# Encoder layer with mLSTM and dilated attention: another DRAM layout of the attention queries and keys, and loads of 128 partitions for wide attention units

## The chip, the cores and the metric

The program runs on one core of a Trainium2 chip. The time is device microseconds of one execution; of several executions the median is given. Times inside the program come from one profiled execution. PE is TensorE, DVE VectorE, ACT ScalarE, POOL GpSimd, SP the engine that does nothing but issue transfers (DMA).

## The reference

One layer of a bidirectional encoder is applied to two sequences, a prompt of 1024 tokens and a sample of 512, both 1024 wide, with the same weights. A common projection feeds an mLSTM branch (4 heads of 256) and an attention branch of three groups (window, dilation) with 8 heads of 64 each; both are gated, projected, merged, projected again and normed. The part that the change touches is the attention's queries and keys:

```python
A_PATTERNS = ((128, 1), (512, 4), (2048, 16))
...
for g, (win, dil) in enumerate(A_PATTERNS):
    o, mx, den = dilated_group(qkv[:, :, 0, g] * (A_HEAD_DIM ** -0.5), qkv[:, :, 1, g], qkv[:, :, 2, g],
                               dil, win // (2 * dil), rel_table[:, g])
...
logits = jnp.einsum('bghnqe,bghnke->bghnqk', qr, kb) + bias[:, None]
logits = jnp.where(mask, logits, -jnp.inf)
mx = jnp.max(logits, axis=-1)
p = jnp.exp(logits - mx[..., None])
o = jnp.einsum('bghnqk,bghnke->bghnqe', p, vb)
```

## The kernel before

The program first projects the prompt (A) and stores what the branches need in DRAM, then runs the branches of A and of the sample (B). During the branches PE is kept busy with the remaining dense products ("fill"): the sample's projection and the output projections.

*Projection of the prompt.* Columns are made in units of 128 (two heads of 64), two units at a time, by seven products of half size (`unit_pair`, products `d<-Hh,phla` and `phlb` at L212 to L214, 19 us a pair). Their weights `pw_raw` are loaded by SP at L692, split into a high and a low part by ACT and DVE (L678, L679) and summed by POOL (L697 to L715). `att_unit` (L770) takes the 24 query and key units, queries (0 to 11) first. For groups 0 and 1 it makes a high part (`hi`, a copy) and a low part (`lo`, the rest), and stores each as 128 rows of 1024 floats into the DRAM tensor `aqk_a` (L222, 512 KB a store). Group 2 has one part only. The sample's units go to `aqk_b` from tiles `sw` while the mLSTM of A runs.

*Attention.* `attend` (L1801) goes through 12 units: unit u is group u // 4, heads 2 (u % 4) and the next. A unit is *wide* when its sequence by residue is longer than 128: groups 0 and 1 of the prompt (units 0 to 7) and group 0 of the sample (units 0 to 3). A wide unit makes the logits of a tile with four products (L1695, `lg<-V0a,Q` and so on): for each head, the query tile, 64 rows of the high part and 64 of the low part in one tile of 128 rows, with a key tile of the same high part twice, and again with a key tile of the low part beside zeros. So `att_load` (L1484) fills, per head, a query tile `Q` from two places of 64 rows, the key tile `V0a` or `V1a` with the same 64 rows in both halves, and half of the tile `V0b` or `V1b` with the low part: five loads of 64 rows a head, ten a unit. Even units use V0, odd ones V1.

*Order of the transfers.* In the branches PE and SP run in the order in which the code is written; DVE, ACT and POOL are ordered by the compiler's scheduler. `att_load` puts its loads into a list (`queue`, L241). `spread(rounds)` sets how many of them go out per step (the length of the list over the rounds, rounded up), `tick` (L234) issues that many at each step, and `need` (L247) issues the rest of a group when its unit begins. All go through `fetch` (L253) to SP. Stores of results wait in a second list (`put`, `flush`, L228). A unit's loads are asked for from the second step of the unit before it. The first unit's loads are asked for during the mLSTM's last head, and stand there ahead of that head's gate loads (`X<-G_a`) in the same list. The fill's weights (`wraw`, L264) go through SP or POOL.

Of the kernel before, what the change touches and what calls it, by code (L numbers as in the profile page):

```python
# [22 lines left out]
F32 = mybir.dt.float32  # L23
# [6 lines left out]
P = 128  # L30
# [9 lines left out]
DILS = (1, 4, 16)  # L40
# [33 lines left out]
class Tokens:  # L74


    def __init__(self, dram, S, x, y, name):
        self.S, self.x, self.y, self.n, self.nblk, self.name = S, x, y, S // P, S // BLK, name
        t = lambda shape, what, dt=F32: dram.tile(shape, dt, name=f"{what}_{name}")
        self.qk = t([16, P, S], "qk")  # L80
        self.vs = t([2, S, D], "vs")
        self.G = t([8, P, S], "G")
        self.aqk = t([2, 24, P, S], "aqk")
        self.av = t([S, 1536], "av")
        self.az = t([4, P, S], "az")
        self.gt = t([2, 8, P, S], "gt")
        self.rw = t([8, self.n, 2, P], "rw")
        self.ym = t([12, P, S], "ym")
        self.og = t([S, 3, 4, OW], "og")


class Rot:
# [91 lines left out]
class Net:  # L184
# [585 lines left out]
    def att_unit(self, j, c, T, w):  # L770

        nc, S = self.nc, T.S
        keys, g = j >= 12, j % 12 // 4
        if g == 2:
            x = w()
            nc.scalar.activation(x.rearrange("p (r i) -> p r i", i=64), c.rearrange("p (i r) -> p r i", i=64), AF.Copy,
                                 scale=1.0 if keys else 0.125)
            self.put(("aqk", T.S, j), T.aqk[0, j], x, x)
            return
        dil = min(DILS[g], S // P)  # L780
        hi, lo = w(F32R), w(F32R)
        if g == 0 and not keys:
            parts = [(hi[:, :S - 64], lo[:, :S - 64], c[:, 64:]), (hi[:, S - 64:], lo[:, S - 64:], c[:, :64])]
        elif not keys and S // dil > P:
            by = lambda z: z.rearrange("p (r i) -> p r i", r=dil)
            x, n = c.rearrange("p (i r) -> p r i", r=dil), S // dil - 64
            parts = [(by(hi)[:, :, :n], by(lo)[:, :, :n], x[:, :, 64:]), (by(hi)[:, :, n:], by(lo)[:, :, n:], x[:, :, :64])]
        else:
            by = lambda z: z.rearrange("p (r i) -> p r i", r=dil)
            parts = [(by(hi), by(lo), c.rearrange("p (i r) -> p r i", r=dil))]  # L790
        for h, _, x in parts:
            nc.scalar.activation(h, x, AF.Copy, scale=1.0 if keys else 0.125)
        for h, l, x in parts:
            nc.vector.scalar_tensor_tensor(l, x, 1.0 if keys else 0.125, h.bitcast(F32), op0=OP.mult, op1=OP.subtract)
        self.put(("aqk", T.S, j), T.aqk[0, j], hi.bitcast(F32), hi)
        self.put(("aqk", T.S, j), T.aqk[1, j], lo.bitcast(F32), lo)


    def short_input(self, ps, xt):
# [684 lines left out]
    def att_load(self, T, u):  # L1484

        nc = self.nc
        g, pr = divmod(u, 4)
        S, n, dil = T.S, T.n, min(DILS[g], T.n)
        wide = S // dil > P
        A, B = slice(0, 64), slice(64, P)
        half = lambda x, i: x[:, i % 2 * 2 * S:(i % 2 + 1) * 2 * S]
        if g == 2:
            return self.compact_load(T, u)
        if S == BLK:
            if u == 0:  # L1500
                self.qs, self.avs = self.take("Q0"), self.take("X1", F32)
            q, v = half(self.qs, u), half(self.avs, u // 2)
            keys = lambda: [x for z in [self.take(f"V{u % 2}a")] for x in (z[:, :2 * S], z[:, 2 * S:])]
        else:
            if pr % 2 == 0:
                self.avs = self.take(f"K{u // 2 % 2}", F32)
            q, v = self.take(f"Q{u % 2}"), self.avs
            keys = lambda: [self.take(f"V{u % 2}{x}") for x in "ab"]
        q = q.rearrange("p (a s) -> p a s", a=2)
        v = v.rearrange("p (n c) -> p n c", c=256)  # L1510
        qd, kd = T.aqk[:, u], T.aqk[:, u + 12]
        if wide:
            kk = self.narrow.get((T, "wide", u % 2)) or [x.rearrange("p (h s) -> p h s", h=2) for x in keys()]
            for hh, rows in enumerate((A, B)):
                self.queue(("att", u), ("aqk", S, u), q[rows, hh].bitcast(F32), qd[0, rows])
                self.queue(("att", u), ("aqk", S, u), q[(B, A)[hh], hh].bitcast(F32), qd[1, rows])
                other = (B, A)[hh]
                for i, to in ((0, A), (0, B), (1, rows)):
                    self.queue(("att", u), ("aqk", S, u + 12), kk[i][to, hh].bitcast(F32), kd[i, rows])
                if (T, "wide", u % 2) not in self.narrow:  # L1520
                    self.zeros.append(lambda x=kk[1][other, hh]: nc.gpsimd.memset(x.bitcast(F32), 0.0))
            self.narrow[T, "wide", u % 2] = kk
            k = [x[:, hh] for x in kk for hh in range(2)]
        else:
            new = (T, u % 2) not in self.narrow
            if new:
                self.narrow[T, u % 2] = [x.rearrange("p (n b s) -> p n b s", n=n, b=2) for x in keys()]
            k = self.narrow[T, u % 2]
            self.queue(("att", u), ("aqk", S, u), q.bitcast(F32), qd.rearrange("a p s -> p a s"))
            for side, rows in enumerate((A, B)):  # L1530
                for i in range(2):
                    if new:
                        nc.gpsimd.memset(k[i][rows, :, 1 - side].bitcast(F32), 0.0)
                    self.queue(("att", u), ("aqk", S, u + 12), k[i][rows, :, side].bitcast(F32), kd[i, rows].rearrange("p (n s) -> p n s", s=P))
        if pr % 2 == 0:
            c0 = 512 * g + 256 * (pr // 2)
            x = S // dil // P
            for r in range(dil):
                self.queue(("att", u), ("av", S), v[:, r * x:(r + 1) * x],
                           T.av[:, c0:c0 + 256].rearrange("(x p r) c -> r p x c", p=P, r=dil)[r])  # L1540
        return [q[:, 0], q[:, 1]], k, v

    def compact_load(self, T, u):

        nc, S, pr = self.nc, T.S, u % 4
        q = self.qs[:, u % 2 * 2 * S:][:, :S].bitcast(F32) if S == BLK else self.take(f"Q{u % 2}", F32)[:, :S]
        new = (T, "compact", u % 2) not in self.narrow
        if new:
            x = [self.take(f"V{u % 2}{x}", F32) for x in ("a" if S == BLK else "ab")]
            self.narrow[T, "compact", u % 2] = [z[:, i * 2 * S:(i + 1) * 2 * S].rearrange("p (h s) -> p h s", h=2)  # L1550
                                                for i, z in ((0, x[0]), (S == BLK, x[-1]))]
        k, v = self.narrow[T, "compact", u % 2]
        if new:
            self.queued += self.values_of(T, u, v)
        self.queue(("att", u), ("aqk", S, u), q, T.aqk[0, u])
        for hh in range(2):
            rows = slice(64 * hh, 64 * hh + 64)
            for z in (k, v) if new else ():
                nc.gpsimd.memset(z[rows, 1 - hh], 0.0)
            self.queue(("att", u), ("aqk", S, u + 12), k[rows, hh], T.aqk[0, u + 12, rows])  # L1560
        return q, k, v

    def values_of(self, T, u, v):
# [938 lines left out]
```

## Time and profile before

| what | value |
|---|---|
| median of 3 runs | 2199.57 us (2198.99 to 2202.0) |
| the profiled execution's own time | 2196.68 us |
| its span, first to last instruction | 2194.8 us |
| granted PE clock | 0.999 |
| PE busy | 2180.1 us, 99% |
| DMA | 390.42 MB, mean 178 GB/s |
| queue of SP (q1): busy share of the 16 DMA engines | 40.5% |
| queue of POOL (q0) | 14.2% |

The profile's lines give an engine, a line of the program, and the tiles as out<-in. "SPq" is SP issuing a transfer; "x2" counts merged instructions. A DMA row of the issue view gives the count, the KB of one and the median time from issue to landing. A wait row reads "who waited <- for whom: total, times, longest".

### The profile page before, as it was taken

The page shows a single profiled execution, that of the slowest core. Times are in us where ns is not written, and L with a number is a line of the kernel's source. Part 1 is how long each engine was busy: PE and PEld are TensorE (multiplying, and loading weights), DVE is VectorE, ACT ScalarE, POOL GpSimd, SP SyncE. Part 2 cuts the span into 40 slices and gives each one's busy share as a digit, 9 for nine tenths or more (in the row PEclk, how much of TensorE's full clock was granted, in tenths as well). Part 3 has the DMA queues.
Part 4 walks back from the last instruction along what each step waited for, and adds up shares of the span by engine and source line. Part 5 has one row for each costly group of instructions (what it writes and reads, how often), then busy time and mean ns, then how long its engine had stood idle before and what let it go on. Part 6 is the DMA issues. An engine that isn't in the chain of part 4 may idle for free.

```text
span 2194.8 us, 34409 instructions
## 1 busy us (share of the span) xinstructions
PE 2180.1 (99%) x11962; PEld 1883.1 (86%) x11962; DVE 1460.9 (67%) x2970; ACT 1088.8 (50%) x2246; POOL 706.5 (32%) x994
## 2 busy tenths in 40 slices
PE   9999999999999999999999999999999999999998
PEld 8999888888888888888888889999788888888887
DVE  7775565657787555547888765574667855666673
ACT  7332243344444333446777656666755544554332
POOL 1000432333333222326776650011045522232331
PEclk9999999999999999999999999999999999999999
DMA  3842443433333222366646569997678786776772
GB/s 126 196 116 80 154 165 135 173 106 112 109 115 109 75 86 96 135 217 239 211 155 228 147 191 248 246 244 198 197 238 279 240 282 209 232 258 183 237 244 106
DMA packets 207640, 390.42 MB, mean 178 GB/s; under 512 B 37513, under 2 KB 121161, under 8 KB 207466
## 3 DMA queue, kind: packets, MB, share of 16 engines
q1 hardware_dynamic: 176584, 276.15, 40.5%
q0 software_dynamic: 27280, 99.48, 14.2%
q10 hardware_dynamic: 3602, 12.59, 1.4%
q8 instruction: 95, 1.56, 0.3%
q14 instruction: 79, 0.65, 0.1%
HBM read 274.70 MB, written 113.44 MB: 177 GB/s over the span
## 4 chain that ended last, share of the span: by engine, by line
PE 90%; DMA 4%; DVE 2%; issue 1%; ACT 1%; POOL 1%; SPq 0%; DVEq 0%; POOLq 0%; ACTq 0%
PE d L214 14%; PE d L212 14%; PE d L213 14%; PE dense L212 11%; PE dense L214 11%; PE dense L213 11%; PE lg L1695 1%; PE pt L1725 1%; PE num L212 1%; PE num L214 1%; PE num L213 1%; PE o L1768 1%; PE num L1390 1%; PE a L1097 1%; PE kv L212 1%
## 5 line engine op out<-in xcount | busy, mean ns | idle before, releaser
L212 PE MATMUL dense<-H,wh 128*128 128x512 f32 x664 | 269.4, 406 | 0.0
L213 PE MATMUL dense<-H,wh 128*128 128x512 f32 x664 | 260.4, 392 | 0.0
L214 PE MATMUL dense<-H,wl 128*128 128x512 f32 x664 | 260.3, 392 | 0.0
L213 PE MATMUL d<-Hl,phla 128*128 128x512 f32 x608 | 236.5, 389 | 0.0
L214 PE MATMUL d<-Hh,phla 128*128 128x512 f32 x608 | 236.5, 389 | 0.0
L212 PE MATMUL d<-Hh,phla 128*128 128x512 f32 x608 | 236.5, 389 | 0.0
L281 DVE TENSOR_TENSOR wl<-wraw,wh 128x1024 fp32r<-128x1024 f32 (+1 forms) x121 | 150.1, 1241 | 49.3 <-ACT wh L275 49.0
L214 PE MATMUL d<-Hh,phlb 128*128 128x512 f32 x456 | 177.4, 389 | 0.0
L212 PE MATMUL d<-Hh,phlb 128*128 128x512 f32 x456 | 177.4, 389 | 0.0
L213 PE MATMUL d<-Hl,phlb 128*128 128x512 f32 x456 | 177.4, 389 | 0.0
L275 ACT ACTIVATE wh<-wraw 128x1024 fp32r<-128x1024 f32 (+1 forms) x124 | 128.2, 1035 | 65.6 <-PE dense L213 21.9
L214 PEld LDWEIGHTS dense<-H,wl 128*128 128x128 f32 x664 | 124.7, 188 | 28.1
L697 POOL TENSOR_TENSOR psum_w<-pw_raw 128x512 f32<-128x512 f32 x38 | 55.3, 1455 | 283.3 <-DMA pw_raw<-w_in 266.0
L214 PE MATMUL d<-vhi,Hl 128*128 128x322 f32 x448 | 140.5, 314 | 0.5 <-DVE Hl L432 0.3
L212 PE MATMUL d<-vhi,Hh 128*128 128x322 f32 x448 | 140.3, 313 | 0.1
L213 PE MATMUL d<-vlo,Hh 128*128 128x322 f32 x448 | 139.6, 312 | 0.0
L212 PEld LDWEIGHTS dense<-H,wh 128*128 128x128 f32 x664 | 125.1, 188 | 16.5 <-issue 1.2
L213 PEld LDWEIGHTS dense<-H,wh 128*128 128x128 f32 x664 | 125.3, 189 | 14.7
L1714 DVE CUSTOM_DVE_ANT_0 ls<-lg,bias 128x256 f32<-128x256 f32 (+2 forms) x240 | 78.8, 352 | 85.5 <-PE lg L1695 63.7
L212 PEld LDWEIGHTS d<-Hh,phla 128*128 128x128 f32 x608 | 114.1, 188 | 23.7
L213 PEld LDWEIGHTS d<-Hl,phla 128*128 128x128 f32 x608 | 114.1, 188 | 23.7
L214 PEld LDWEIGHTS d<-Hh,phla 128*128 128x128 f32 x608 | 114.1, 188 | 23.6
(635 smaller groups left out, 5811.1 us busy)
## 6 DMA issues: line engine op xcount, KB each, us to landing
pw_raw<-w_in SPq DMA_DIRECT2D x76, 512.0 KB, 4.3
wraw<-w_in SPq DMA_DIRECT2D x63, 512.0 KB, 4.3
aqk_a<-pwk SPq DMA_DIRECT2D x40, 512.0 KB, 3.5
wraw<-w_pm POOLq DMA_DIRECT2D x24, 512.0 KB, 5.5
wraw<-w_out POOLq DMA_DIRECT2D x24, 512.0 KB, 4.0
aqk_b<-sw SPq DMA_DIRECT2D x40, 256.0 KB, 6.2
wraw<-w_v POOLq DMA_DIRECT2D x22, 430.0 KB, 7.2
qk_a<-pwk SPq DMA_DIRECT2D x16, 512.0 KB, 2.6
```

The source lines that it names most:

```text
L212: nc.tensor.matmul(out, lh, rh, start=start, stop=False, **kw)
L213: nc.tensor.matmul(out, lh, rl, start=False, stop=False, **kw)
L214: nc.tensor.matmul(out, ll, rh, start=False, stop=stop, **kw)
L275: high = nc.scalar.activation(hi[:, :n], raw[:, :n], AF.Copy)
L281: low = (self.lows or nc.vector).tensor_sub(lo[:, :n], raw[:, :n], hi[:, :n].bitcast(F32))
L697: self.nc.gpsimd.tensor_add(s[:, 0], ws[1][:, 0], ws[1][:, 1])
L1097: nc.tensor.matmul(p[:, c - c0], kT[:, ct, c * P:(c + 1) * P], qT[:, ct, c * P:(c + 1) * P], start=ct == 0, stop=ct == 1)
L1390: nc.tensor.matmul(pn, hi[:, j], z[:, c1], start=j == 0 and z is v[0], stop=False)
L1695: nc.tensor.matmul(lg[:, hh], q[hh][:, qs], z.rearrange("p (n j) -> p n j", j=P)[:, pair], start=z is k[hh], stop=z is not k[hh])
L1714: nc.vector.tensor_tensor_reduce(out=ls[rows, hh], in0=ts["lg"][hh][rows, of], in1=bt[rows, hh, by], scale=1.0, scalar=NEG, op0=OP.add, op ...
L1725: nc.tensor.transpose(pp[:, hh * nk + x], ts["ls"][:, hh, x * P:(x + 1) * P], self.ident)
L1768: nc.tensor.matmul(of(hh, 0, P), vh(kt[x], hh), pt[:, hh * len(kt) + x], start=x == 0, stop=x == len(kt) - 1)
```

## The change

`aqk` becomes a tensor of four planes of 64 rows for each unit. For a wide query the planes are: high part of head 0, low part of head 0, low part of head 1, high part of head 1, so that the two planes that a query tile takes lie beside each other. For the rest they are: high part of both heads, low part of both heads. `plane(j, i)` gives the place of unit j's part i; the high part of a wide query is planes 0 and 3, which do not lie beside each other.

```diff
-        self.aqk = t([2, 24, P, S], "aqk")
+        self.aqk = t([24, 4, 64, S], "aqk")
...
+    def wide(self, g):
+        return self.S // min(DILS[g], self.n) > P
+
+    def plane(self, j, i):
+        x = self.aqk[j]
+        if j < 12 and self.wide(j // 4):
+            return x[1:3] if i else x[0::3]
+        return x[2 * i:2 * i + 2].rearrange("a p s -> (a p) s")
...
-        self.put(("aqk", T.S, j), T.aqk[0, j], hi.bitcast(F32), hi)
-        self.put(("aqk", T.S, j), T.aqk[1, j], lo.bitcast(F32), lo)
+        self.put(("aqk", T.S, j), T.plane(j, 0), hi.bitcast(F32), hi)
+        self.put(("aqk", T.S, j), T.plane(j, 1), lo.bitcast(F32), lo)
...
-        qd, kd = T.aqk[:, u], T.aqk[:, u + 12]
         if wide:
+            qd, kd = T.aqk[u], T.aqk[u + 12]
             kk = self.narrow.get((T, "wide", u % 2)) or [x.rearrange("p (h s) -> p h s", h=2) for x in keys()]
+            for hh in range(2):
+                self.queue(("att", u), ("aqk", S, u), q[:, hh].bitcast(F32), qd[2 * hh:2 * hh + 2].rearrange("a p s -> (a p) s"))
+                self.queue(("att", u), ("aqk", S, u + 12), kk[0][:, hh].bitcast(F32),
+                           kd[hh].unsqueeze(0).to_broadcast([2, 64, S]))
             for hh, rows in enumerate((A, B)):
-                self.queue(("att", u), ("aqk", S, u), q[rows, hh].bitcast(F32), qd[0, rows])
-                self.queue(("att", u), ("aqk", S, u), q[(B, A)[hh], hh].bitcast(F32), qd[1, rows])
-                other = (B, A)[hh]
-                for i, to in ((0, A), (0, B), (1, rows)):
-                    self.queue(("att", u), ("aqk", S, u + 12), kk[i][to, hh].bitcast(F32), kd[i, rows])
+                self.queue(("att", u), ("aqk", S, u + 12), kk[1][rows, hh].bitcast(F32), kd[2 + hh])
```

The other units and `compact_load` read the same data from their new places in as many loads as before. PE's order is the same. SP issues 48 transfers fewer, and they change shape. In the store stage SP's rows around the first pairs of query units are, before (a shape is that of the side with more dimensions):

```order
L692 DMA pw_raw<-w_in 128x1024 x3
L222 DMA aqk_a<-pwk 128x1024 x4
L692 DMA pw_raw<-w_in 128x1024 x2
L222 DMA aqk_a<-pwk 128x1024 x4
L692 DMA pw_raw<-w_in 128x1024 x2
```

and of the changed program, in which the lines are nine further down:

```order
L701 DMA pw_raw<-w_in 128x1024 x3
L231 DMA aqk_a<-pwk 2x64x1024 x2
L231 DMA aqk_a<-pwk 128x1024 x2
L701 DMA pw_raw<-w_in 128x1024 x2
L231 DMA aqk_a<-pwk 2x64x1024 x2
L231 DMA aqk_a<-pwk 128x1024 x2
L701 DMA pw_raw<-w_in 128x1024 x2
```

The stores of the high parts of the eight wide query units now have two blocks of 64 rows as their target; nothing else moved. In the prompt's attention SP's rows for unit 2 (its bias tables, loads into `Q`, `V0a`, `V0b` and the values `K`, between stores of results `og_a` and of the fill `vs_b`) are, before:

```order
L253 DMA bias_12410<-erow 128x256 x2
L253 DMA Q_12718<-aqk_a 64x1024 x2
L253 DMA V0a<-aqk_a 64x1024 x2
L228 DMA og_a<-ot_12419 128x4x132
L228 DMA vs_b<-sw_7817 128x414
L228 DMA vs_b<-sw_7814 128x414
L253 DMA V0b<-aqk_a 64x1024
L253 DMA Q_12718<-aqk_a 64x1024 x2
L253 DMA V0a<-aqk_a 64x1024 x2
L253 DMA V0b<-aqk_a 64x1024
L253 DMA K_12717<-av_a 128x8x256
```

and of the changed program:

```order
L262 DMA bias_12406<-erow 128x256 x2
L262 DMA Q_12710<-aqk_a 128x1024
L262 DMA V0a<-aqk_a 128x1x1024
L237 DMA og_a<-ot_12415 128x4x132
L237 DMA vs_b<-sw_7817 128x414
L237 DMA vs_b<-sw_7814 128x414
L262 DMA Q_12710<-aqk_a 128x1024
L262 DMA V0a<-aqk_a 128x1x1024
L262 DMA V0b<-aqk_a 64x1024 x2
L262 DMA K_12709<-av_a 128x8x256
```

Ten loads became six; those of `V0a` read 64 rows twice (128x1x1024 is their target, the source is 2x64x1024 with a step of 0), and the low parts come last. In the same way `X<-G_a` of the last mLSTM head moves ahead of one weight load on SP. On DVE one piece of the sample's attention, where the low parts of the weights (`Q<-wraw`) and of the fill's rows (`K`, `H`) are made beside the logits, reads before:

```order
L1716 TENSOR_SCALAR nm<-ot 128x2
L2046 TENSOR_TENSOR K_18109<-sraw,K_18108 128x512
L281 TENSOR_TENSOR Q_18061<-wraw_7696,Q_18061 128x1024
L1714 ISA ls,ot<-lg,bias_18084 128x256
L1714 ISA ot 128x1
L1714 ISA ls,ot<-lg,bias_18084 128x256
L1714 ISA ot 128x1
L1731 COPY pts<-pt 128x512
L2046 TENSOR_TENSOR K_18109<-ymr_18065,K_18108 128x512
```

and of the changed program:

```order
L1725 TENSOR_SCALAR nm<-ot 128x2
L290 TENSOR_TENSOR Q_18025<-wraw_7696,Q_18025 128x1024
L2055 TENSOR_TENSOR K_18073<-sraw,K_18072 128x512
L2055 TENSOR_TENSOR K_18073<-ymr_18029,K_18072 128x512
L1723 ISA ls,ot<-lg,bias_18048 128x256
L1723 ISA ot 128x1
L1723 ISA ls,ot<-lg,bias_18048 128x256
L1723 ISA ot 128x1
L1740 COPY pts<-pt 128x512
```

The second `K` row goes ahead of the logits, the first one place back behind the weight.

More of the change, by code (lines that the diff above doesn't have):

```diff
@@ L777, in att_unit @@
                                  scale=1.0 if keys else 0.125)
-            self.put(("aqk", T.S, j), T.aqk[0, j], x, x)
+            self.put(("aqk", T.S, j), T.plane(j, 0), x, x)
             return
@@ L1510, in att_load @@
         v = v.rearrange("p (n c) -> p n c", c=256)
-        qd, kd = T.aqk[:, u], T.aqk[:, u + 12]
         if wide:
+            qd, kd = T.aqk[u], T.aqk[u + 12]
             kk = self.narrow.get((T, "wide", u % 2)) or [x.rearrange("p (h s) -> p h s", h=2) for x in keys()]
+            for hh in range(2):
+                self.queue(("att", u), ("aqk", S, u), q[:, hh].bitcast(F32), qd[2 * hh:2 * hh + 2].rearrange("a p s -> (a p) s"))
+                self.queue(("att", u), ("aqk", S, u + 12), kk[0][:, hh].bitcast(F32),
+                           kd[hh].unsqueeze(0).to_broadcast([2, 64, S]))
             for hh, rows in enumerate((A, B)):
-                self.queue(("att", u), ("aqk", S, u), q[rows, hh].bitcast(F32), qd[0, rows])
-                self.queue(("att", u), ("aqk", S, u), q[(B, A)[hh], hh].bitcast(F32), qd[1, rows])
-                other = (B, A)[hh]
-                for i, to in ((0, A), (0, B), (1, rows)):
-                    self.queue(("att", u), ("aqk", S, u + 12), kk[i][to, hh].bitcast(F32), kd[i, rows])
+                self.queue(("att", u), ("aqk", S, u + 12), kk[1][rows, hh].bitcast(F32), kd[2 + hh])
                 if (T, "wide", u % 2) not in self.narrow:
-                    self.zeros.append(lambda x=kk[1][other, hh]: nc.gpsimd.memset(x.bitcast(F32), 0.0))
+                    self.zeros.append(lambda x=kk[1][(B, A)[hh], hh]: nc.gpsimd.memset(x.bitcast(F32), 0.0))
             self.narrow[T, "wide", u % 2] = kk
@@ L1528, in att_load @@
             k = self.narrow[T, u % 2]
-            self.queue(("att", u), ("aqk", S, u), q.bitcast(F32), qd.rearrange("a p s -> p a s"))
+            self.queue(("att", u), ("aqk", S, u), q.bitcast(F32), T.aqk[u].rearrange("(a h) p s -> (h p) a s", a=2))
             for side, rows in enumerate((A, B)):
@@ L1533, in att_load @@
                         nc.gpsimd.memset(k[i][rows, :, 1 - side].bitcast(F32), 0.0)
-                    self.queue(("att", u), ("aqk", S, u + 12), k[i][rows, :, side].bitcast(F32), kd[i, rows].rearrange("p (n s) -> p n s", s=P))
+                    self.queue(("att", u), ("aqk", S, u + 12), k[i][rows, :, side].bitcast(F32), T.aqk[u + 12, 2 * i + side].rearrange("p (n s) -> p n s", s=P))
         if pr % 2 == 0:
@@ L1554, in compact_load @@
             self.queued += self.values_of(T, u, v)
-        self.queue(("att", u), ("aqk", S, u), q, T.aqk[0, u])
+        self.queue(("att", u), ("aqk", S, u), q, T.plane(u, 0))
         for hh in range(2):
@@ L1559, in compact_load @@
                 nc.gpsimd.memset(z[rows, 1 - hh], 0.0)
-            self.queue(("att", u), ("aqk", S, u + 12), k[rows, hh], T.aqk[0, u + 12, rows])
+            self.queue(("att", u), ("aqk", S, u + 12), k[rows, hh], T.aqk[u + 12, hh])
         return q, k, v
```

## The prediction

> **What bounds the kernel now.** I read the page's busy shares first, then the chain, then who TensorE (PE) waited for, then the stages in a table by windows. The page says:
>
> ```profile
> span 2194.8 us, 34409 instructions
> PE 2180.1 (99%) x11962; PEld 1883.1 (86%) x11962; DVE 1460.9 (67%) x2970; ACT 1088.8 (50%) x2246; POOL 706.5 (32%) x994
> PE 90%; DMA 4%; DVE 2%; issue 1%; ACT 1%; POOL 1%; SPq 0%; DVEq 0%; POOLq 0%; ACTq 0%
> ```
>
> PE is busy 99% of the span and carries 90% of the chain that ended last. So a transfer is worth only the time for which PE stands still for it. The view of waits has all of it that concerns this change in three rows (total, times, longest, in us), of which the first is the start of the program:
>
> ```profile
> PE d L2254 <- DMA Hh<-prew: 3.3, 1, 3.3
> PE lg L1695 <- DMA V0b<-aqk_a: 0.4, 1, 0.4
> PE lg L1695 <- DMA V1b<-aqk_a: 0.2, 1, 0.2
> ```
>
> PE's idle time is 2194.8 - 2180.1 = 14.7 us in all, so nothing here can gain much. What can be lost is not bounded that way: PE runs in written order, and a late operand stops it. The table by windows shows how much room the DMA engines have (us, then busy time by engine; the last three columns are PE's clock, the mean busy share of the 16 DMA engines, and GB/s). The first row is the stage that stores the attention queries, the next two are the prompt's attention, the last the sample's:
>
> ```profile
> 256.00:327.00 71.00, 71.00 (x315) 58.80 (x314) 46.77 (x56) 27.51 (x33) 21.76 (x15) 1.00 0.46 170
> 1306.00:1330.00 24.00, 23.72 (x159) 20.72 (x159) 15.68 (x56) 16.83 (x44) 4.09 (x6) 1.00 0.85 225
> 1330.00:1476.00 146.00, 145.36 (x1177) 136.97 (x1176) 91.75 (x373) 94.38 (x287) 11.15 (x19) 1.00 0.98 252
> 1779.00:1799.00 20.00, 20.00 (x103) 16.99 (x102) 12.86 (x34) 12.63 (x28) 6.51 (x13) 1.00 0.93 302
> ```
>
> The prompt's attention keeps all 16 DMA engines about full (0.98). There an uneven spread over the engines would show at once; in the first stage half is free (0.46).
>
> **The change, part by part.** The rows of the issue view say what goes away and what bulk stays (KB of one, us from issue to landing):
>
> ```profile
> aqk_a<-pwk SPq DMA_DIRECT2D x40, 512.0 KB, 3.5
> Q<-aqk_a SPq DMA_DIRECT2D x32, 256.0 KB, 6.6
> V0a<-aqk_a SPq DMA_DIRECT2D x20, 256.0 KB, 6.4
> V1a<-aqk_a SPq DMA_DIRECT2D x20, 256.0 KB, 7.9
> Q<-qk_a SPq DMA_DIRECT2D x8, 512.0 KB, 7.0
> ```
>
> Twelve wide units (eight of the prompt, four of the sample) have ten loads each before and six after: 48 issues fewer on SP, the same bytes. SP is not on the chain (0%), so the issues themselves are worth nothing. The query loads become loads of 128 whole rows; 512 KB in 7.0 us (`Q<-qk_a`) beside 256 KB in 6.6 us says that they are no dearer per byte. The gain is the two waits above. In time from one PE start to the next they are 0.6 us each: in the rows below, four products of a unit's first tile stand 0.12 us apart until the last comes 0.67 us after the third.
>
> ```profile
> 1452.12 0.28 PE L1695 MATMUL lg<-V0a,Q 128*128 128x256 f32 x1
> 1452.23 0.28 PE L1695 MATMUL lg<-V0b,Q 128*128 128x256 f32 x1
> 1452.35 0.28 PE L1695 MATMUL lg<-V0a,Q 128*128 128x256 f32 x1
> 1453.02 0.39 PE L1695 MATMUL lg<-V0b,Q 128*128 128x256 f32 x1 [0.40 <-DMA V0b<-aqk_a]
> ```
>
> So about -1.2 us if every transfer is spread as evenly as now.
>
> The other side is the shape of 36 transfers, which the program's order on SP shows: 16 + 8 key loads whose source pattern is two copies of 64 rows (the repeat is the outer step), and 8 + 4 query stores written as 2x64 rows. All other transfers of these two tensors have an outer count of 64 or 128. I take it that a transfer is cut among the DMA engines along its outermost count, so that these 36 run on **two engines of 16**, and always the same two. The trace of before bears on this in one place, eight small loads at its start:
>
> ```profile
> L354 SPq DMA_DIRECT2D tb<-rel x8: 310/366/507, 90.4 to 95.6; - x8
> ```
>
> Four of them have 16 rows and four 15. Every transfer is counted home in 16 steps. In the trace's semaphore events each of the four 15-row loads shows one step alone at 0.5 to 0.7 us after its issue and the other 15 later; the 16-row loads show no early step. That is one engine with nothing to do, so the spread follows the row count. No row of before prices an outer count of two, so its price is bounded by other rows.
>
> The Trainium skill, "DMA: Bandwidth & Descriptors", section "Why a DMA increments its semaphore by 16 and not by 1", says that the number of engines is the largest one up to 16 that divides the outermost count (over one) of both patterns, and that the queues of SP take the lowest-numbered ones; its "Rules for kernel authors" names a leading repeat of c copies as confined to c engines. The 15-row loads agree; by this rule the sum is the one below. The same table's rule on two transfers to partition halves (use one over 128 partitions instead) speaks for the query loads; no run here shows it yet, and by it alone the sum would be the -1.2 us.
>
> *Price of one such transfer.* Half of 512 KB, 262144 bytes, passes each of two engines. A busy engine moves 170/(0.46 x 16) = 23.1 GB/s in the store stage and 252/(0.98 x 16) = 16.1 GB/s in the attention: 11.3 to 16.3 us, where 3.5 to 7.9 us stand now. Until then everything that is queued behind on SP's queue waits for its own small share on these two engines.
>
> *The store stage.* A pair of units takes 292.37 - 273.33 = 19.04 us of PE:
>
> ```profile
> 252.88 1.71 SPq L692 DMA_DIRECT2D pw_raw<-w_in  x2
> 262.70 1.07 ACT L678 ACTIVATE phla<-pw_raw 128x1024 fp32r<-128x1024 f32 x1 [4.89 <-PE d L214]
> 273.33 0.39 PE L212 MATMUL d<-Hh,phla 128*128 128x512 f32 x1
> 275.29 3.02 SPq L222 DMA_DIRECT2D aqk_a<-pwk  x4
> 292.37 0.39 PE L212 MATMUL d<-Hh,phla 128*128 128x512 f32 x1
> ```
>
> Four pairs store two wide queries each: 2 x 11.3 = 22.7 us on the two engines, beside 0.46 x 19.04 = 8.8 us of other work less 2.8 us (the old share of these stores: 65536 bytes at 23.1 GB/s). That is 28.6 us in 19.04, a deficit of 9.6 us a pair, 38 us for four. Behind the stores stand the weight loads of the pair after next (L692). They are issued 20.4 us ahead of use; ACT splits them 10.6 us ahead, so some 10 us of delay is covered. The drain after the fourth pair, which stores nothing wide for two pairs, covers more. I take +20 us; ends 0 and +38.
>
> *The prompt's attention.* Its units follow each other every (1476.45 - 1330.14)/6 = 24.4 us:
>
> ```profile
> 1310.59 1.11 SPq L253 DMA_DIRECT2D Q<-aqk_a  x2
> 1316.60 0.45 SPq L253 DMA_DIRECT2D V1b<-aqk_a  x1
> 1330.14 0.28 PE L1695 MATMUL lg<-V1a,Q 128*128 128x256 f32 x1
> 1476.45 0.28 PE L1695 MATMUL lg<-V1a,Q 128*128 128x256 f32 x1
> ```
>
> Two repeated loads a unit are 22.7 us on the two engines at the low price. Other work there is 252 x 24.4/16 = 384 KB at 23.1 GB/s = 16.6 us, less 2.8 for the old key loads: 36.5 us in 24.4, a deficit of 12.1. Unit 1's loads start at 1310.6 and land 22.7 + 3.5 us later, 1336.8, which is 7 us late; six more units make 7 + 6 x 12.1 = 80 us. At the high price it is 32.6 + 0.98 x 24.4 - 4.1 = 52.4 us, a deficit of 28.0, and 17 + 6 x 28 = 185 us. If other queues' share of the two engines is only half of 13.8 us, it is 7 + 6 x 5.2 = 38. I take 90, near the low price, because the other 14 engines stand idle meanwhile; above 80, because SP keeps only so many transfers under way and then waits for one to land, which it does already:
>
> ```profile
> SPq L253 <- DMA Q<-aqk_a: 5.3, 6, 1.5
> ```
>
> *The rest.* The sample's key loads have half the bytes, two of 5.7 us (131072 bytes at 23.1 GB/s) a unit, and they are issued 20 us ahead of use, so 0 (end +20):
>
> ```profile
> 1779.62 1.87 SPq L253 DMA_DIRECT2D V1a<-aqk_b  x3
> 1799.51 0.36 PE L1695 MATMUL lg<-V1a,Q 128*128 128x256 f32 x1
> ```
>
> The first unit's loads run under the mLSTM (+0, end +10). Fewer issues also bring the gate loads of the last mLSTM head forward and move a few DVE, ACT and POOL instructions by one to five places; the row in reach is PE's one wait there,
>
> ```profile
> 1814.81 0.50 PE L213 MATMUL dense<-K,wh 128*128 128x512 f32 x1 [0.21 <-DVE K L2046]
> ```
>
> which the new DVE order serves earlier: 0, within 0.4 us either way.
>
> *Sum.* 20 + 90 = +110 us. The profiled execution took 2196.7 us (2194.8 of span and 1.9 around it): 2306.7. The median of the three runs, 2199.57, lies 2.9 us above it, so I predict 2309.6, rounded **2310 us**.
>
> **The rivals.**
> - *Spread evenly.* The stores and repeated loads use all 16 engines after all, and only the -1.2 us is left: 2195.5, on the median's scale 2198.4, not slower. Mechanism: rows are dealt out one by one, whatever the outer count. It decides from the point where a `V0a<-aqk_a` of 512 KB lands within some 9 us. For it: 64-row transfers land like 128-row ones. Against it: the 15-row loads.
> - *Two engines, but hidden in the attention.* Loads are asked for up to 20 us ahead, and if the other queues' work on the two engines is thin, only the store stage pays: 2199.6 + 20 = 2220. Against it: 0.98 of DMA share.
> - *SP's queue as a whole falls to the high price*: 38 + 185 = 223 us, 2423. For it: in-order issue with few transfers under way, so that stores and tables wait as well. Against it: the 16.1 GB/s contain contention by 16 full engines.
>
> **How the numbers follow.** Forecast 0.73, even spread 0.09, hidden 0.08, high price 0.10. Forecast's own ends: 38 + 0 gives 2238; 185 + 38 + 20 gives 2443, which belongs to the last rival. The range 2230 to 2410 leaves out the two low rivals and half of the high one. A measurement of this kernel can tell about 0.2%, 4.4 us, from no change. Faster by that needs more idle time than the change touches: 0.02, noise within the even spread; same 0.07; slower 0.91.
>
> **What would show it.** Right: `V0a<-aqk_a` and `V1a<-aqk_a` rows of 512 KB landing after 11 us or more; stores of 2x64 rows likewise; PE waiting for `pw_raw` or `phla` near 290 to 340 us and for `aqk_a` loads at each unit's start; units 35 us or longer; a lower DMA share and GB/s from 1310 on with the same bytes in all. Wrong: landings of 4 to 9 us and PE still at 99%. If stores are slow but loads are not, the outer count matters on the written side alone, and the time is about 2220.

## The result and the profile after

The changed kernel takes **2328.9 us** (median of 6 runs, 2326.61 to 2332.69), the kernel before 2199.28 us on the same chip (2196.86 to 2202.0): ratio 1.0591, 95% interval 1.0577 to 1.0604. The profiled execution took 2328.85 us. The page of the changed kernel, its span, PE's row, PE's clock in 40 slices, and the chain by engine:

```profile
span 2327.0 us, 34334 instructions
PE 2210.1 (95%) x11962; PEld 1904.8 (82%) x11962; DVE 1464.0 (63%) x2970; ACT 1088.7 (47%) x2246; POOL 708.1 (30%) x994
...
PEclk9999999999999999999999988788999999999999
...
DMA packets 206367, 390.40 MB, mean 168 GB/s; under 512 B 36241, under 2 KB 119889, under 8 KB 206194
...
PE 77%; DMA 14%; DVE 2%; issue 2%; SPq 2%; ACT 1%; POOL 1%; DVEq 0%; POOLq 0%; ACTq 0%
```

The bytes are the same; the span is 132.2 us longer. PE's idle time rose from 14.7 to 2327.0 - 2210.1 = 116.9 us, and its busy time by 30.0 us at the same 11962 products: the second part is the clock (below). The view of PE's waits says who was late (total, times, longest):

```profile
PE lg L1704 <- DMA V1b<-aqk_a: 37.4, 3, 15.0
PE pt L1787 <- ACT oT L1780: 16.2, 1, 16.2
PE lg L1704 <- DMA V0b<-aqk_a: 15.5, 2, 10.0
PE lg L1704 <- DMA K<-av_a: 14.6, 1, 14.6
PE num L221 <- ACT X L1203: 7.9, 3, 6.2
PE d L221 <- ACT phla L687: 5.4, 2, 4.7
```

The table by windows, for the stretches quoted of before (the later ones hold other work now, since all is shifted):

```profile
256.00:327.00 71.00, 65.07 (x276) 52.31 (x275) 38.81 (x48) 22.58 (x28) 17.08 (x12) 0.95 0.36 130
1330.00:1476.00 146.00, 103.23 (x743) 95.32 (x741) 56.67 (x209) 63.89 (x184) 7.00 (x13) 0.85 0.56 164
```

In the attention the mean share of the DMA engines fell from 0.98 to 0.56 and PE from 145 to 103 us of 146. If two engines are busy all the time, the other 14 are so for (0.56 x 16 - 2)/14 = 0.50 of it (an estimate): half of their time they stand idle while PE waits for two.

PE's products come in the same order in both traces, so the start of one and the same product can be subtracted. That shift, at the ends of stages (us of the trace before), divides the loss:

| stage | shift at its start and end | loss | predicted |
|---|---|---|---|
| query stores, to 480 | 0.1, 9.0 | 9 | 20 |
| to 1231 (the sample's query stores) | 9.0, 11.2 | 2.2 | not priced |
| mLSTM's last head, to 1306 | 11.2, 21.3 | 10.1 | 0, end 10 |
| prompt's attention, 1326.5 to 1506 | 20.6, 121.8 | 101.2 | 90 |
| sample's attention, 1779 to 1968 | 123.0, 133.3 | 10.3 | 0, end 20 |
| all | 132.3 at the end | 132.3 | 110 |

**The two engines themselves.** The trace records every step of the semaphore that counts a transfer home; a transfer's records stand between its issue and the next issue on that semaphore. An ordinary transfer leaves 16. In the changed kernel 36 transfers leave 3, and they are the 36 that the prediction named (16 + 8 key loads, 8 + 4 stores); every other transfer of SP leaves 16 or more. Since the issue view reckons with 16 for each, it has no landing times for SP here. Some of the records (us after the issue; runs named e are described below):

```
trace, issue at                               records
before  275.29 store, 128 rows                16: from 2.5 to 4.2
after   276.05 store, 2x64 rows                3: 0.9, 18.2, 18.2
after   301.91 store, 2x64 rows                3: 0.9, 17.2, 17.2
after  1331.16 repeated load V1a, 2x64 rows    3: 1.0, 17.3, 17.7
after  1332.42 the next one                    3: 0.9, 32.2, 32.4
after  1345.00 load V1b, 64 rows              16: 14 from 5.6 to 6.0, then 21.4, 21.6
e4     1371.18 load, 4 blocks of 32 rows       5: 1.0, 11.7, 12.8, 12.9, 13.7
e5     1355.58 load, 8 blocks of 16 rows       9: 1.1, then 8 from 7.7 to 9.5
e6     1295.94 repeated load, POOL's queue    16: 14 from 2.6 to 3.8, then 17.4, 17.6
e6     1296.82 the next one                   16: 12 from 2.6 to 3.1, then 17.5, 17.6, 18.1, 18.3
```

The count must reach 16, so the one record at 1 us stands for the 14 engines that have nothing to do, and the two late ones for those that carry the transfer. The next repeated load lands 1332.42 + 32.4 - 1331.16 - 17.7 = 16.0 us after the first: they queue on the same two. The V1b load behind them is spread over 16, has 14 shares home at 6.0 us and waits 15.6 us more for the two. The Trainium skill, "DMA: Bandwidth & Descriptors", section "Why a DMA increments its semaphore by 16 and not by 1", says that SP writes the count of the unused engines at once and each used engine adds one when its data have landed; the records agree, with 3 for two engines, 5 for four and 9 for eight.

### The profile page after: what moved, and what is told of

It is laid out like the page before. It is cut to its first block, busy times and chain, and to the rows that moved or that the text cites. A ratio compares the mean times of both kernels' runs of the same rounds, so it can differ in the third digit from the quotient of the medians.

```text
span 2327.0 us, 34334 instructions
## 1 busy us (share of the span) xinstructions
PE 2210.1 (95%) x11962; PEld 1904.8 (82%) x11962; DVE 1464.0 (63%) x2970; ACT 1088.7 (47%) x2246; POOL 708.1 (30%) x994
## 3 DMA queue, kind: packets, MB, share of 16 engines
q0 software_dynamic: 27280, 99.48, 13.5%
## 4 chain that ended last, share of the span: by engine, by line
PE 77%; DMA 14%; DVE 2%; issue 2%; SPq 2%; ACT 1%; POOL 1%; DVEq 0%; POOLq 0%; ACTq 0%
PE d L223 12%; PE d L221 12%; PE d L222 12%; PE dense L221 10%; PE dense L222 9%; PE dense L223 9%; DMA V1b<-aqk_a 2%; DMA aqk_a<-pwk 2%; DMA wraw<-w_in 2%; DMA V0b<-aqk_a 2%; SPq L262 2%; DMA vs_b<-sw 1%; DMA V0a<-aqk_a 1%; PE lg L1704 1%; DMA og_a<-ot 1%
## 5 line engine op out<-in xcount | busy, mean ns | idle before, releaser
L1727 ACT ACTIVATE ls<-ls,nm 128x256 f32<-128x256 f32 (+1 forms) x192 | 87.3, 456 | 139.3 <-DVE nm L1725 80.0
L221 PEld LDWEIGHTS dense<-H,wh 128*128 128x128 f32 x664 | 125.5, 189 | 16.5 <-issue 1.2
L222 PEld LDWEIGHTS dense<-H,wh 128*128 128x128 f32 x664 | 125.7, 189 | 14.7
```

The lines of the kernel that those rows point to most:

```text
L221: nc.tensor.matmul(out, lh, rh, start=start, stop=False, **kw)
L222: nc.tensor.matmul(out, lh, rl, start=False, stop=False, **kw)
L1727: self.held = self.held[-3:] + [nc.scalar.activation(ls[:, hh], ls[:, hh], AF.Exp, bias=nm[:, hh:hh + 1], accum_out=ot[:, 128 + hh:129 + hh])]
```

## The experiments

Each run is compared with the kernel before on the same chip. "Both split" (e3) is the base from which the two parts are counted.

### e1: only the stores in two blocks

```diff
-                self.queue(("att", u), ("aqk", S, u + 12), kk[0][:, hh].bitcast(F32),
-                           kd[hh].unsqueeze(0).to_broadcast([2, 64, S]))
+                for to in (A, B):
+                    self.queue(("att", u), ("aqk", S, u + 12), kk[0][to, hh].bitcast(F32), kd[hh])
```

> The changed kernel with each repeated key load written as two loads of 64 rows (outer count 64); the query stores stay 2x64 rows. If an outer count of two confines a transfer to two engines, only what the trace of the changed kernel shows outside the attention and outside the mLSTM's last head is left: 8.9 us in the store stage and about 2 us near 1000 to 1020 us, where the sample's queries have been stored: 2199 + 11 = 2210 us (2206 to 2216), with no wait of PE over 1 us behind 1310 us. If the loads were dear for another reason (rows of the new layout, the order of issue), the attention stays long: over 2300 us.

Measured: 2208.72 us, before 2198.11; ratio 1.0045 (1.0031 to 1.0059). The loss behind 1310 us is gone; the store stage has its shift of 10.6 us. PE's longest wait is again there:

```profile
PE d L221 <- ACT phla L687: 5.4, 2, 4.7
```

### e2: only the repeated loads

```diff
-        self.put(("aqk", T.S, j), T.plane(j, 0), hi.bitcast(F32), hi)
+        if not keys and T.wide(g):
+            for a, rows in ((0, slice(0, 64)), (3, slice(64, P))):
+                self.put(("aqk", T.S, j), T.aqk[j, a], hi[rows].bitcast(F32), hi)
+        else:
+            self.put(("aqk", T.S, j), T.plane(j, 0), hi.bitcast(F32), hi)
```

> The changed kernel with each 2x64-row query store written as two stores of 64 rows; the repeated key loads stay. Two engines: the store stage loses nothing and the rest of the loss stays, 2329 - 11 = 2318 us (2313 to 2323); stores of 512 KB no longer appear, the 64-row ones land within 6 us. If the late loads were an effect of what the stores had left behind on a queue, the attention would recover: near 2200 us.

Measured: 2316.05 us, ratio 1.0536 (1.0522 to 1.055). The store stage has no loss (shift 1.0 us from start to 960), the mLSTM's last head keeps its 10.3 us and the prompt's attention 99.9. So those 10 us at the mLSTM's end belong to the first unit's loads.

### e3: both split

Both edits together.

> Both undone; what stays of the change is the new order of the query halves in DRAM and query loads of 128 rows (24 issues fewer than before). By the two engines everything is spread again: the 1.2 us of two waits may go, 2198 us (2194 to 2202), nothing that can be told from no change. If the 128-row query loads or the new order in DRAM cost something by themselves, over 2204 us.

Measured: 2194.47 us (11 runs), before 2198.11 (15 runs); ratio 0.9984 (0.9975 to 0.9993). That is 3.6 us under the kernel before, the fastest version here: a gain of 0.16%, which the interval only just tells from none. The two waits of which the prediction spoke are gone: there the shift moves by -0.51 and -0.55 us. At the place where the last of four products came 0.67 us after the third, this trace has

```profile
1451.82 0.28 PE L1708 MATMUL lg<-V0a,Q 128*128 128x256 f32 x1
1451.94 0.28 PE L1708 MATMUL lg<-V0b,Q 128*128 128x256 f32 x1
1452.05 0.28 PE L1708 MATMUL lg<-V0a,Q 128*128 128x256 f32 x1
1452.17 0.28 PE L1708 MATMUL lg<-V0b,Q 128*128 128x256 f32 x1
```

Counted from here the stores cost 2208.7 - 2194.5 = 14.2 us and the loads 2316.1 - 2194.5 = 121.6; together 135.8, where the whole change costs 2328.9 - 2194.5 = 134.4. The parts add up to within the 1 to 3 us by which the chips differ.

### e4 and e5: four and eight engines

Stores split, and the repeated load replaced by one of the same size with another outer count and no repeat (shown for 4; for 8, `b=2` and 16 rows). Both bring other rows than the attention needs.

```diff
-                           kd[hh].unsqueeze(0).to_broadcast([2, 64, S]))
+                           kd.rearrange("a (b p) s -> (a b) p s", b=1)[:, :32])
```

> Stores split; each repeated key load is replaced by one load of 512 KB whose source is 4 blocks of 32 rows of the same unit's key planes: outer count 4, no repeat. It brings wrong rows, so the logits and all behind them are not the reference's. If the engines follow the outer count, four engines carry each: a unit on them takes 26.0 to 29.0 us (half of the two loads' 18.4 to 24.4 us beside 19.8 to 13.8 us of other work) where 38.2 are measured with two engines and 24.4 are needed; 1.6 to 4.6 us a unit over seven: 2221 us (2205 to 2240), the loads landing after 6 to 12 us, with 12 steps of their count early and 4 late. If it is the reading of the same rows twice that is dear, 2199 us and landings of 4 to 8 us. If it is any source with an outer block count below 16, whatever its number, 2318 us.

> Stores split; each repeated key load is replaced by one load of 512 KB whose source is 8 blocks of 16 rows of the same unit's key planes: outer count 8. It brings wrong rows, so the logits and all behind them are not the reference's. From the runs with two engines (38.2 us a unit in the changed kernel) and four (24.4 + 5.4 = 29.8 us a unit) the busiest engine's unit is 21.4 us of other work and 16.8/k x 2 of these loads (8.4 at four engines); with eight 21.4 + 4.2 = 25.6 us, 1.2 more than is needed: over six units, with some us for the first, 2194.5 (both split) + 10 = 2204 us (2199 to 2211), 8 steps early and 8 late, 5 to 9 us to land. If eight engines are enough to hide them, 2194.5 us (2191 to 2198). If only 16 count as spread, as slow as with four: 2244 us.

Measured: e4 2244.25 us, ratio 1.0207 (1.0193 to 1.0221), 4 us outside its range; e5 2210.99, ratio 1.0058 (1.0039 to 1.0077), against a before of 2196.78. The number of late steps is 4 and 8, as the rows above show, so the count of the outermost dimension decides and not the repeat. The windows of the prompt's attention, of e4 and of e5, stand between 0.56 and full:

```profile
1330.00:1476.00 146.00, 117.78 (x891) 110.20 (x892) 65.26 (x259) 71.72 (x216) 6.89 (x13) 0.89 0.72 195
```

```profile
1330.00:1476.00 146.00, 139.67 (x1106) 131.30 (x1105) 85.60 (x350) 87.92 (x269) 8.05 (x15) 0.98 0.89 235
```

Four engines were expected to cost less because the estimate gave the loads some cover. There is none to speak of; see the table at e7.

### e7: one of two loads repeated

Stores split; the load of the first head stays repeated, that of the second is split.

```diff
-                self.queue(("att", u), ("aqk", S, u + 12), kk[0][:, hh].bitcast(F32),
-                           kd[hh].unsqueeze(0).to_broadcast([2, 64, S]))
+                if hh == 0:
+                    self.queue(("att", u), ("aqk", S, u + 12), kk[0][:, hh].bitcast(F32),
+                               kd[hh].unsqueeze(0).to_broadcast([2, 64, S]))
+                else:
+                    for to in (A, B):
+                        self.queue(("att", u), ("aqk", S, u + 12), kk[0][to, hh].bitcast(F32), kd[hh])
```

> Stores split; only the first of a unit's two repeated key loads stays, the second is two loads of 64 rows. If the loss is a backlog of bytes on two engines, half of the bytes there give what four engines gave: 21.4 + 8.4 = 29.8 us a unit, 2244 us (2225 to 2260). If the loss is only the landing time of one late load (16 to 18 us, with loads asked for some 20 us ahead), it is hidden: 2197 us (2192 to 2204).

Measured: 2251.41 us, ratio 1.0244 (1.0227 to 1.0262). So a backlog of bytes on the two engines fits (2244 us was expected), a mere late landing does not (2197). With this run the loss can be set against one quantity, the share of these loads' bytes on the busiest engine beyond an even sixteenth:

| run | share on the busiest engine - 1/16 | us above both split | us per unit of share |
|---|---|---|---|
| e5, eight engines | 0.125 - 0.0625 = 0.0625 | 16.5 | 264 |
| e4, four | 0.1875 | 49.8 | 266 |
| e7, half on two, half on 16 | 0.2188 | 56.9 | 260 |
| e2, two | 0.4375 | 121.6 | 278 |

Within some 10% the loss is proportional to the excess bytes on the busiest engine. (e5 and e7 ran on a chip on which the kernel before is 1.3 us faster; with that added they give 285 and 266.) No threshold shows, though e5's 16.5 us is known only to some 4 us. In the attention the engines were at 0.98, so little was there to hide it.

### e6 and e8: the other queue

e6 is e2 with the repeated loads issued by POOL (`nc.gpsimd`) instead of SP; e8 is e3 with the same 64-row loads issued by POOL.

```diff
-                           kd[hh].unsqueeze(0).to_broadcast([2, 64, S]))
+                           kd[hh].unsqueeze(0).to_broadcast([2, 64, S]), nc.gpsimd)
```

> Stores split; the repeated key loads keep their outer count of two, but GpSimd issues them on its own queue instead of SP. If being confined to the same two engines is a trait of SP's queue and the other queue takes turns among the engines, each load still takes 10 to 18 us on its two engines, but not behind the last one and not ahead of all else: hidden, 2197 us (2193 to 2206), with PE's waits for aqk_a under 3 us in all. If that queue deals out rows over 16 engines, the same time with landings of 4 to 9 us. If two engines, and the same two, also serve this queue, 2316 us as with SP's.

Measured: 2224.78 us, ratio 1.0121 (1.0102 to 1.014). Both forecasts missed, at 2197 and at 2316. In the records above two loads issued 0.9 us apart land nearly together, 17.6 and 18.3 us after their issues and not 16 us apart: they are on different engines. PE's single waits are small, but transfers that are spread evenly still have a share on some busy pair. The issue views show it, first e6, then e3:

```profile
Q<-aqk_a SPq DMA_DIRECT2D x20, 512.0 KB, 10.3
...
V0a<-aqk_a POOLq DMA_DIRECT2D x8, 512.0 KB, 21.6
V1a<-aqk_a POOLq DMA_DIRECT2D x8, 512.0 KB, 19.6
```

```profile
Q<-aqk_a SPq DMA_DIRECT2D x20, 512.0 KB, 6.2
V0a<-aqk_a SPq DMA_DIRECT2D x20, 256.0 KB, 6.9
V1a<-aqk_a SPq DMA_DIRECT2D x20, 256.0 KB, 7.4
```

The same section of the Trainium skill, "DMA: Bandwidth & Descriptors", says that on POOL's queue all 16 engines report, whatever the shape, and that a transfer on fewer takes the next ones in turn. The 16 records and the common landing agree. It does not make the 30 us foreseeable, so one more run told queue from shape:

> As the run before it on GpSimd's queue (2224.8 us, 30 us above the 2194.5 us with both split on SP's queue), but with each repeated load written as two loads of 64 rows, still issued by GpSimd. If those 30 us come from transfers that sit on two engines each, wherever these lie (in that run evenly spread loads of queries landed late in their last two to four steps), they go: 2197 us (2193 to 2203). If they come from the queue or from GpSimd standing at the loads' waits, they stay or grow with twice as many issues: 2218 to 2240 us.

Measured: 2198.66 us, ratio 1.0002 (0.9992 to 1.0011), and the issue view has

```profile
V0a<-aqk_a POOLq DMA_DIRECT2D x16, 256.0 KB, 6.3
V1a<-aqk_a POOLq DMA_DIRECT2D x16, 256.0 KB, 7.5
```

The queue costs about 4 us (2198.7 - 2194.5); 26 of e6's 30 us are the two-engine shape, even where the pair changes from load to load.

## Why the prediction was nearly right, step by step

**Mechanism: right.** From four small loads of 15 rows it concluded that a transfer is cut along its outermost count and that two blocks mean two engines, always the same. The records and e4, e5 and e7 show it. *Spread evenly* is out (e3 is what it would have been, at 2194.5 against 2198.4 foretold), *hidden in the attention* too (e2). *The high price everywhere* foretold 223 us of loss and got 132.3.

**The gain: about right.** The two waits went (e3), and 3.6 us is more than the 1.2 counted, by rows too small to follow one by one: the shift of e3 moves by -1.4 us in the prompt's attention, by -0.5 at 1638.70 of the trace before and by -0.4 at 1814.81, a wait on DVE's order that was given 0 within 0.4.

**Price of a transfer: about right for a unit, left incomplete where loads were counted alone.** 11.3 to 16.3 us was the estimate for 512 KB. The first store, with none of its kind ahead, took 13.0 us, and the second of a pair landed 9.9 to 11.2 us after the first; where both of a unit's repeated loads were under way, the second landed 13.5 to 18.5 us after the first. These spacings contain the shares of other transfers on the same two engines, so they are not the bare price. A whole unit tells more: it took 38.2 us (see below), where 36.5 were foretold at the low price and 52.4 at the high. By the prediction's own count a unit brings each of the two engines 2 x 262144 bytes and 384 - 64 KB of other work; in 38.2 us this is 22 GB/s (an estimate), close to the 23.1 of the low price. So "near the low price" held for a unit. What failed is the sum for unit 1, 22.7 + 3.5 us: it let nothing else pass through the two engines, and the second load landed 33.6 us after the issue of the first (1331.16 to 1364.8). The sample's loads, of half the bytes, were counted alone as well: they landed 8.2 to 11.0 us apart, not 5.7, and their stage lost 10.3 us where 0 was taken.

**Store stage: 9 instead of 20, and the late operand was another.** The prediction let the weights `pw_raw` queue behind the stores, as issued 20.4 us ahead of use. That was a misreading: in the trace before, the split at 281.74 waits for the semaphore of the load issued at 252.88, and PE uses it at 292.37, 39.5 us after the issue. So in the changed kernel they were late but not too late: those issued at 273.33 landed 9.7 us later, at 283.0, and were split at 308.05. ACT's order of time in the changed kernel shows the operand that was late:

```profile
294.35 0.66 ACT L801 ACTIVATE pwk<-c 128x256 fp32r<-128x256 f32 x1 [11.17 <-DMA aqk_a<-pwk]
294.91 1.04 ACT L687 ACTIVATE phla<-psum_w 128x1024 fp32r<-128x1024 f32 x1
...
319.23 0.65 ACT L801 ACTIVATE pwk<-c 128x256 fp32r<-128x256 f32 x1 [10.12 <-DMA aqk_a<-pwk]
319.79 1.04 ACT L687 ACTIVATE phla<-psum_w 128x1024 fp32r<-128x1024 f32 x1
```

The buffer `pwk` for the next high part is free only when the store two units earlier has left, 18.2 us after its issue. ACT stands before it, and the next weights' split `phla`, in ACT's order behind it, comes too late for PE: 4.7 us at 320.88, the wait for `phla` in the table of waits. That the stores crowd the two engines was right, and the buffer was the missed link. The deficit was too large as well: the four pairs' stores ran from 256.36 to the last landing at 355.2, 98.8 us in 4 x 19.04 = 76.2, 5.7 us a pair and not 9.6.

**First unit: 10.1 us, at the end given, not at 0.** Its two repeated loads, issued at 1243.25 and 1255.21, stood in front of a weight load of the fill (`wraw`), of which 14 shares were home after 7.6 us and the two on the same two engines after 22.4 and 23.1. ACT's split of this weight stands in ACT's order before a step of the mLSTM (`X`) for which PE waits. ACT's row, and the chain of the changed kernel:

```profile
1279.08 1.06 ACT L284 ACTIVATE wh<-wraw 128x1024 fp32r<-128x1024 f32 x1 [6.76 <-DMA wraw<-w_in]
...
1255.88 23.12 DMA wraw<-w_in
1279.17 0.86 issue
1280.04 0.58 ACT sw L765
...
1281.44 0.38 ACT X L1203
1281.86 0.58 PE num L221
```

The prediction asked only whether the loads themselves came in time; what queues behind them was named for the stores and forgotten here. e2 keeps this loss, e1 does not.

**Prompt's attention: 101.2 instead of 90.** Units followed each other every 38.2 us (last late products at 1366.01 and, six units later, 1595.12), foretold 36.5. Unit 1 came 15.2 us late, foretold 7:

```profile
1350.72 0.28 PE L1704 MATMUL lg<-V1a,Q 128*128 128x256 f32 x1
1366.01 0.55 PE L1704 MATMUL lg<-V1b,Q 128*128 128x256 f32 x1 [15.01 <-DMA V1b<-aqk_a]
```

The late one is V1b, a load that is spread evenly but lies behind both repeated ones. The same holds for the row `K<-av_a` (14.6 us) of the table of waits, which names the wrong load:

```profile
1477.68 0.58 PE L1704 MATMUL lg<-V0b,Q 128*128 128x256 f32 x1 [14.64 <-DMA K<-av_a]
```

This product does not read `K`. It waits for two semaphores, and the one that came last, at 1477.64, is that of the `V0b` load issued at 1456.68, of which 14 shares were home after 4.7 us and the last after 21.0. So `V0b` and `V1b` account for 37.4 + 15.5 + 14.6 = 67.5 us of PE's waits. One large wait is not for `aqk_a`: `pt <- ACT oT` (16.2) goes back to a store of the fill. ACT's `sw` waits until it has left, and `oT` stands behind `sw`, as the chain of the changed kernel has it:

```profile
1499.82 16.50 DMA vs_b<-sw
1516.82 0.38 ACT sw L857
1517.20 0.49 ACT oT L1780
```

This is what the prediction called the small share on these two engines. Without the 10 us added for SP the prediction's sum for this stage was 80: of the 21 us beyond it, 8 are unit 1's, 10 the 1.7 us in each of the six that follow, and 3 come after the last wait, while the clock recovers.

**Sum.** 110 foretold, 132.3 measured: -11 in the store stage, +10 for the mLSTM's last head, +11 for the prompt's and +10 for the sample's attention, and 2 for the sample's query stores, which were listed and not priced. In times 2310 us were foretold and 2328.9 measured. That the sum is so near is partly luck: the store stage, 11 too high, hides a third of the 33 that the other stages were too low.

## What to carry to other kernels

Before two transfers are joined into one, look at the outermost dimension of both sides: here one dimension of two at the front cost 130 us, and the same data in twice as many transfers of 64 rows nothing. A stage whose DMA engines are as full as here (0.98) has hardly any cover for an uneven transfer, and the victim was mostly an even one queued behind it; the price followed the excess of bytes on the busiest engine. For each transfer that becomes slower, ask also what waits for its source buffer, not only for its data.

## What the runs showed of the hardware beyond that

*SP's issue itself stands.* With two two-engine transfers ahead, the issue of the next transfer often takes several us. SP's rows of the changed kernel in the store stage and before unit 1:

```profile
256.36 11.28 SPq L231 DMA_DIRECT2D aqk_a<-pwk  x4
...
1332.98 14.10 SPq L262 DMA_DIRECT2D V1b<-aqk_a  x2
```

In the first group the third issue alone takes 8.10 us, in the second the first V1b takes 11.97, while ordinary issues mostly take 0.3 to 0.6. Each of these two long issues ends shortly before the older of the two transfers lands (266.39 and 269.4, 1344.95 and 1348.9). Everything later on SP's queue starts that much later; which part of the 132 us comes from this and which from the engines' backlog is not separated by these runs.

*PE's clock falls in a wait.* After the wait of 15 us before 1366.01 the granted clock is at half for 2 us and recovers within 4; before it and afterwards it is 1.00:

```profile
1344.00:1350.00 6.00, 6.00 (x59) 5.46 (x58) 4.52 (x18) 4.89 (x13) 1.09 (x2) 1.00 0.75 188
...
1366.00:1368.00 2.00, 1.99 (x8) 1.81 (x9) 0.62 (x3) 0.00 (x0) 0.00 (x0) 0.50 0.43 139
1368.00:1370.00 2.00, 2.00 (x9) 1.87 (x9) 0.91 (x4) 1.00 (x4) 0.00 (x0) 0.63 0.14 57
1370.00:1372.00 2.00, 2.00 (x14) 1.95 (x13) 0.98 (x6) 1.13 (x6) 0.00 (x0) 1.00 0.16 61
```

So each long wait costs some 2 us more than it lasts. That is why busy time rose by 30.0 us with the same products (it is a modelled time; by the shift, starts after the waits fall back by 1 to 3 us each).
